# Reordering the scaling of x's last four row tiles, the unread products and one weight split in the modulation stage of a hybrid decoder kernel

## The chip, the cores and the metric

The kernel runs on one core of one Trainium2 chip. The metric is device microseconds of one execution. Before the change, three runs took 1377.65 us in the median (1375.61 to 1378.57).

## The reference, cut to what matters

One decoder layer on x of 1024 rows by 1024 columns, float32. The whole layer feeds on `h`, which the kernel makes first:

```python
mod = jax.nn.silu(c) @ ada_w + ada_b
shift, scale, gate = jnp.split(mod, 3, axis=-1)
h = rms_norm(x, norm_w) * (1 + scale[:, None, :]) + shift[:, None, :]
proj = h @ w_in
...
merged = jax.nn.sigmoid(g_a) * (y_a @ w_proj_a) + jax.nn.sigmoid(g_b) * (y_b @ w_proj_b)
return x + gate[:, None, :] * (merged @ w_out)
```

Between `proj` and `merged` lie a chunked spatial gating mixer and a state space mixer. A last `rms_norm` follows. All that comes after `h` is the same work, in the same order on every engine, before and after the change.

## The kernel before, in words

The change lies in the first stage (some 76 us), which makes `h` transposed, in column blocks of 128, and multiplies each block with the first 288 columns of `w_in` that the kernel wants early.

**Norm of x.** x lies in eight row tiles of 128 rows, x0 to x7. `square(t)` lets ScalarE sum the squares of tile t (one pass over 128x1024, then a readout). `factors(t)` makes the factor 1/sqrt(mean + eps): a small VectorE instruction on one column (L380), then a power on GpSimd (L381). `normed(t, half, V)` multiplies one half of the tile's columns, 128x512, with the factor on VectorE (L388). Half 0 holds columns 0 to 511, half 1 the rest. The factors of x0 to x3 are taken one after the other ahead of the stretch that is changed here.

**Blocks.** There are eight steps n; step n makes block k = KS[n] with KS = (0, 4, 1, 5, 2, 6, 3, 7), so step 0 reads half 0 of x's tiles and step 1 reads half 1. For each block: `matvec(n)` multiplies `scz` (the silu of c) with a block of `ada_w` (the tile `aw`) into `pm`, and a copy makes `row` of it; `modulation(n)` turns the row into two columns with TensorE and adds the constants on VectorE, which gives `md` (shift and scale); `transposes(n, h)` transposes four 128x128 pieces of x's tiles (h = 0: x0 to x3, h = 1: x4 to x7) into one PSUM bank `px`, of which there is one; `rows_of_h(n, h)` makes of it and `md` the block `hf` on ScalarE (L308), a high part of it on ScalarE (L309, the cast) and the low part on VectorE (L313); `split_w0(n)` makes the high and low parts of the early weights (`w0h`, `w0d` on ScalarE, `w0l`, `w0d` on VectorE); and `first_products(n)` multiplies, eight products for each h, numbered 1 to 16 in a step.

**Order.** Everything in this stage is kept in the order of the program on its engine. The dictionary that `prepare(n)` returns says after which product of the step before the parts of step n are issued. For step 1 it reads: after the eighth product of step 0 the second half of block 0 (`transposes(0, 1)`, `rows_of_h(0, 1)`) with `matvec(1)` and `split_w0(1)`; after the eleventh `transposes(1, 1)`, `modulation(1)`, `rows_of_h(1, 1)`; after the sixteenth the other half of block 1.

**Unread products.** `warm(n)` issues n products of two constant tiles into a part of PSUM that nothing reads before it is overwritten. The profile shows each of them, as every 128x128 or 32x256 float32 product, as two records.

**Queues.** All loads go through SyncE's queue in the order of the program: x0 to x3, `aw` and `w0r` of step 0, x4 to x7, `aw` and `w0r` of step 1, five small parameters, then `aw` and `w0r` of steps 2 and on. Two `aw` tiles exist, so the load for step n + 2 waits for `matvec(n)`.

Of the kernel before, what the change touches and what calls it, by code (L numbers as in the profile page):

```python
# [35 lines left out]
def hybrid_kernel(  # L36
# [21 lines left out]
    V, A, G, PE = Engine(nc.vector), Engine(nc.scalar), Engine(nc.gpsimd), nc.tensor  # L58
# [31 lines left out]
    def mm(acc, l, r, first=True, last=True):  # L90
        pin(PE.matmul(acc, l, r, start=first, stop=last))  # L91

    def tp(dst, src, idn):
        pin(PE.transpose(dst, src, idn))  # L94

    def f32(t):
        return t.bitcast(F32)
# [61 lines left out]
    def ax(name, tag="pm"):  # L159
        return psum0.tile([P, 512], F32, name=name, tag=tag, bufs=1)  # L160
# [15 lines left out]
    def wide(name, dt=F32):  # L176
        return w4[0].tile([P, S], dt, name=name, tag="w4", bufs=w4[1])


    with tc.tile_pool(name="p0", bufs=1, reuse_waits="tile") as p0:  # L180
# [14 lines left out]
        def hf_tile(k, h):  # L195
            if k not in hf2:
                hf2[k] = wide(f"hf{k}")
            return hf2[k][:, h * 512 : (h + 1) * 512]
# [31 lines left out]
        def split_w0(n):  # L230
            raw, wd, hi, lo = wk[n]
            pin(A.copy(hi, raw[:, NH:W0]))
            pin(A.copy(wd[:, 0:NH], raw[:, 0:NH]))
            pin(V.tensor_sub(lo, raw[:, NH:W0], f32(hi)))
            pin(V.tensor_sub(wd[:, NH:], raw[:, 0:NH], f32(wd[:, 0:NH])))
# [17 lines left out]
        def warm(n):  # L253

            for _ in range(n):
                mm(accs[2][1][:, 0:P], ident, ones)
# [10 lines left out]
        def matvec(n):  # L267

            pms[n] = pm = ax(f"pm{n}")
            for i in range(KT):  # L270
                q = i % 4
                mm(pm[32 * q : 32 * q + 32, 0:256], scz[:, i, :], aw[n][:, i].rearrange("p j c -> p (j c)"),
                   i < 4, i >= 4)
            row = p0.tile([P, 256], F32, name=f"row{n}", tag="row", bufs=2)
            pin(V.tensor_copy(row, pm[:, 0:256]) if n == 0 else A.copy(row, pm[:, 0:256]))
            mds[n] = row

        def modulation(n):

            k, pm, row = KS[n], pms[n], mds[n]  # L280
            for j in range(2):
                mm(pm[:, 256 + j : 257 + j], row[:, j * P : (j + 1) * P], ones[:, 0:1])
            md = p0.tile([P, 2], F32, name=f"md{n}", tag="md", bufs=3)
            pin(V.tensor_add(md[:, 0:1], pm[:, 256:257], par[:, 16 + k : 17 + k]))
            pin(V.scalar_tensor_tensor(md[:, 1:2], pm[:, 257:258], par[:, 24 + k : 25 + k], par[:, 8 + k : 9 + k],
                                       op0=ALU.add, op1=ALU.mult))
            mds[n] = md

        def transposes(n, h):
            k = KS[n]  # L290
            px = pxs[n, h] if n + h == 0 else ax(f"px{n}_{h}", "px")
            for i in range(4):
                tp(px[:, i * P : (i + 1) * P], xt[4 * h + i][:, k * P : (k + 1) * P], ident)
            pxs[n, h] = px

        def rows_of_h(n, h):
            k, md, px = KS[n], mds[n], pxs[n, h]
            if k < 4 and h:
                b12 = wide(f"b12_{k}", F32R)
                hh, hl = b12[:, 0:512], b12[:, 512:1024]  # L300
            else:
                nm = ("b11" if k < 4 else ("b21", "b22")[h])
                hh, hl = bop[nm][0][k % 4], bop[nm][1][k % 4]
            if n + h:
                hfs[k, h] = hf_tile(k, h)
            hf = hfs[k, h]
            if n + h:
                pin(A.activation(hf, px, AF.Identity, scale=md[:, 1:2], bias=md[:, 0:1]))  # L308
                pin(A.copy(hh, hf))  # L309
            else:  # L310
                pin(V.tensor_scalar(hf, px, md[:, 1:2], md[:, 0:1], op0=ALU.mult, op1=ALU.add))
                pin(V.tensor_copy(hh, hf))
            pin(V.tensor_sub(hl, hf, f32(hh)))  # L313
            hhs[n, h] = (hh, hl)
# [52 lines left out]
        def halves(n):  # L367

            return (0, 1) if KS[n] < 4 else (1, 0)
# [5 lines left out]
        def square(t):  # L375
            pin(A.activation(junk, xt[t], AF.Square, accum_out=sq0[:, t : t + 1]))

        def factors(t):
            bs = slice(t, t + 1)
            pin(V.tensor_scalar(sq0[:, bs], sq0[:, bs], 1.0 / D, EPS, op0=ALU.mult, op1=ALU.add))  # L380
            pin(G.tensor_tensor(rs[:, bs], sq0[:, bs], nhalf[:, bs], op=ALU.pow))  # L381

        def normed(t, half, eng):
            part = xt[t][:, half * 512 : (half + 1) * 512]
            if eng is A:
                pin(A.mul(part, part, rs[:, t : t + 1]))
            else:
                pin(V.tensor_scalar_mul(part, part, rs[:, t : t + 1]))  # L388

        for t in range(4):  # L390
            square(t)
            factors(t)
            normed(t, 0, V)
        transposes(0, 0)
        matvec(0)
        split_w0(0)
# [3 lines left out]
        rows_of_h(0, 0)  # L400
        for t in range(4, NCH):
            square(t)
            factors(t)
            normed(t, 0, V)
            if t in (5, 6):
                normed(t - 5, 1, V)
        for t in range(4, NCH):
            normed(t, 1, V)
        for t in (2, 3):
# [2 lines left out]
        def prepare(n):  # L412

            if n == 1:
                return {
                    8: lambda: (warm(6), transposes(0, 1), rows_of_h(0, 1), matvec(1), split_w0(1), warm(5)),
                    11: lambda: (transposes(1, 1), modulation(1), rows_of_h(1, 1)),
                    16: lambda: (transposes(1, 0), rows_of_h(1, 0)),
                }
            a, b = halves(n)  # L420
            return {
                2: lambda: (matvec(n), transposes(n, a)),
                6: lambda: (modulation(n), rows_of_h(n, a)),
                14: lambda: (transposes(n, b), rows_of_h(n, b)),
            }
# [20 lines left out]
        for n in range(KT):  # L446
            todo = prepare(n + 1) if n + 1 < KT else {}
            for at, _ in enumerate(first_products(n), 1):
                if at == 1 and n + 2 < KT:
                    load_aw(n + 2)  # L450
                    load_w0(n + 2)
                if at == 1 and n == 1:
                    load(dsk, d_skip.to_broadcast([P, NH]))
                if at in todo:
                    todo[at]()
                for f, kk in sums.get((n, at), ()):
                    f(kk)
                if at == 2 and 0 < n < KT - 1:
                    split_w0(n + 1)
                if n == 4 and at == 8:  # L460
                    small_parameters()
# [1357 lines left out]
    n = 0  # L1819
# [284 lines left out]
```

## Time and profile before

| | us |
|---|---|
| three runs, median | 1377.65 |
| profiled execution, its own time | 1379.03 |
| its span, first to last instruction | 1377.3 |
| outside the span | 1.7 |
| TensorE busy in the span | 1358.4 |
| VectorE, ScalarE, GpSimd busy | 1058.2, 788.0, 203.1 |

The profiled execution took 1.4 us more than the median of the three runs and 0.5 us more than the slowest of them. All times in the parts below are counted from the start of its span. A row of the timeline names its start, how long the group lasted, the engine, the line, the operation, the tiles (`px<-ident,x`: px is written, ident and x are read) and how many instructions are in the group; the brackets at its end give the time that the engine stood idle before it, and what ended that. PE is TensorE, DVE VectorE, ACT ScalarE, POOL GpSimd, SP SyncE.

### The profile page before, as it was taken

What the parts mean: (1) busy time and instruction counts of PE and PEld (TensorE: products, weight loads), DVE (VectorE), ACT (ScalarE), POOL (GpSimd) and SP (SyncE); (2) the same over time, 40 slices, a digit from 0 to 9 for tenths busy, and PEclk for the clock granted to TensorE, in tenths of its full rate; (3) what the DMA queues carried; (4) which work ended last, traced back from release to release, by engine and by line L of the source; (5) the groups of instructions that cost most, each with busy time, mean ns of one, the idle gap of its engine ahead of it and who ended that gap; (6) DMA issues with size and microseconds to landing.
All of it is one profiled execution on the core that took longest, in us unless ns stands there. A gap on an engine that the chain in (4) does not pass through costs nothing.

```text
span 1377.3 us, 20335 instructions
## 1 busy us (share of the span) xinstructions
PE 1358.4 (99%) x6947; PEld 1121.2 (81%) x6947; DVE 1058.2 (77%) x1793; ACT 788.0 (57%) x1465; POOL 203.1 (15%) x208
## 2 busy tenths in 40 slices
PE   8999999999999999999999999999999999999998
PEld 6778888888888888888878888888888878888886
DVE  5766766888776687778889988567887887778975
ACT  5764456565656656565556655577877744233543
POOL 1000000000000000000000000006898881000012
PEclk9999999999999999999999999999999999999999
DMA  8665532545323346776887886578989959977733
GB/s 266 169 221 163 173 111 93 166 140 164 107 81 123 107 134 176 210 225 206 249 258 231 245 253 180 168 270 310 327 264 315 313 169 296 392 263 285 258 120 123
DMA packets 272364, 286.58 MB, mean 208 GB/s; under 512 B 18780, under 2 KB 215812, under 8 KB 272260
## 3 DMA queue, kind: packets, MB, share of 16 engines
q1 hardware_dynamic: 196100, 214.35, 49.4%
q10 hardware_dynamic: 76160, 70.92, 15.1%
q8 instruction: 55, 0.90, 0.3%
q14 instruction: 49, 0.40, 0.1%
HBM read 198.77 MB, written 86.44 MB: 207 GB/s over the span
## 4 chain that ended last, share of the span: by engine, by line
PE 80%; DVE 6%; DMA 6%; issue 3%; POOL 2%; ACT 1%; SPq 0%; ACTq 0%; POOLq 0%; DVEq 0%
PE x L1721 6%; PE xuz L591 6%; PE xcb L591 5%; PE xx L591 5%; PE yp L1721 5%; PE pma L91 4%; PE xz L591 4%; PE xg L591 4%; PE ou L1964 3%; PE yuz L591 3%; PE vx L703 3%; PE acc L91 3%; PE ycb L591 3%; PE vy L703 2%; PE yx L591 2%
## 5 line engine op out<-in xcount | busy, mean ns | idle before, releaser
L56 POOL TENSOR_SCALAR_AFFINE_SELECT dcy<-dcy 128x1024 f32<-128x1024 f32 x32 | 34.9, 1092 | 778.5 <-DMA yl<-ya_d 733.1
L56 ACT ACTIVATE dcy<-dcy,nacs 128x128 f32<-128x128 f32 x256 | 78.4, 389 | 17.6 <-POOL dcy L56 17.2
L56 ACT ACTIVATE ea<-dcy 64x512 f32<-64x512 f32 x64 | 40.3, 629 | 8.9 <-DMA dcy<-acs_d 8.5
L91 PE MATMUL pma<-yh,wah 128*128 128x512 f32 x128 | 43.0, 417 | 0.0
L91 PE MATMUL pma<-yh,wal 128*128 128x512 f32 x128 | 42.7, 414 | 0.0
L56 POOL TENSOR_TENSOR yz<-y,sl 128x512 f32<-128x512 f32 x32 | 41.9, 1310 | 0.6
L1043 ACT ACTIVATE ac<-ac 128x1024 f32<-128x1024 f32 x32 | 33.9, 1061 | 12.8 <-DVE ac L1041 12.7
L56 DVE TENSOR_TENSOR ym<-yn,ea 128x512 f32<-128x512 f32 (+1 forms) x32 | 19.9, 623 | 27.6 <-PE yn L91 27.5
L56 DVE TENSOR_TENSOR dcy<-dcy,pc 128x1024 f32<-128x1024 f32 x32 | 38.9, 1215 | 2.4 <-PE pc L94 0.9
L91 PE MATMUL pma<-yl,wah 128*128 128x512 f32 x128 | 39.9, 393 | 0.0
L56 POOL TENSOR_TENSOR y<-y,ym 128x512 f32<-128x512 f32 (+1 forms) x32 | 38.4, 1199 | 9.3 <-DVE ym L56 9.2
L1041 DVE SCALAR_TENSOR_TENSOR ac<-c2cb,cwt,ac 128x1023 f32<-128x1023 f32 (+2 forms) x24 | 30.7, 1280 | 6.8 <-ACT ac L1039 6.7
L1041 DVE SCALAR_TENSOR_TENSOR ac<-c2x,cwt,ac 128x1023 f32<-128x1023 f32 (+2 forms) x24 | 30.7, 1279 | 6.1 <-ACT ac L1039 6.0
L91 PE MATMUL yi<-dcy,xd 128*64 128x128 f32 x512 | 35.0, 279 | 0.3 <-DVE xd L56 0.3
L91 PE MATMUL sp<-xe,bn 128*128 128x256 f32 x112 | 32.7, 409 | 0.0
L91 PEld LDWEIGHTS yi<-dcy,xd 128*64 128x64 f32 x512 | 27.3, 136 | 6.4 <-issue 4.4
L2025 POOL TENSOR_TENSOR r<-r,xr 128x512 f32<-128x512 f32 x4 | 6.3, 1588 | 170.2 <-DMA xr<-in_x_dram 169.0
L1041 DVE SCALAR_TENSOR_TENSOR ac<-c1x,cwt,ac 128x1023 f32<-128x1023 f32 (+2 forms) x24 | 30.7, 1277 | 0.7 <-ACT ac L1039 0.7
L1041 DVE SCALAR_TENSOR_TENSOR ac<-c1cb,cwt,ac 128x1023 f32<-128x1023 f32 (+2 forms) x24 | 30.6, 1276 | 0.0
L56 DVE SCALAR_TENSOR_TENSOR yn<-yn,par,rb 128x512 f32<-128x512 f32 x32 | 25.7, 804 | 6.2 <-DMA yn<-yb_d 6.2
L56 DVE SCALAR_TENSOR_TENSOR y<-sl,dskt,yi 128x256 f32<-128x256 f32 x64 | 27.5, 470 | 1.2 <-POOL yz L56 1.2
L91 PEld LDWEIGHTS pma<-yl,wah 128*128 128x128 f32 x128 | 24.0, 188 | 5.4
(2911 smaller groups left out, 4352.0 us busy)
## 6 DMA issues: line engine op xcount, KB each, us to landing
sl<-s_d SPq DMA_DIRECT2D x32, 768.0 KB
s_d<-ac ACTq DMA_DIRECT2D x32, 512.0 KB
dcy<-acs_d SPq DMA_DIRECT2D x32, 512.0 KB
aw<-in_ada_w_dram SPq DMA_DIRECT2D x16, 512.0 KB
vp<-in_w_in_dram SPq DMA_DIRECT2D x32, 256.0 KB
wbr<-in_w_proj_b_dram SPq DMA_DIRECT2D x64, 128.0 KB
wb_d<-wbb ACTq DMA_DIRECT2D x32, 256.0 KB
wb_d<-wbc ACTq DMA_DIRECT2D x32, 256.0 KB
```

The lines of the kernel that those rows point to most:

```text
L56: return lambda *a, **k: tc.keep_in_program_order(f(*a, **k))
L91: pin(PE.matmul(acc, l, r, start=first, stop=last))
L591: pin(PE.matmul(ps, lw[:, k * P : (k + 1) * P], r[k], start=first and n + k == 0, stop=n == 2 and k == 3, skip_group_check=not first))
L703: pin(PE.matmul(ps[j], l[k][:, js], r, start=first and k + m == 0, stop=k == 3 and m == 2, skip_group_check=not first))
L1041: V.scalar_tensor_tensor(ac[:, s:], cc[:, : S - s], conv_wt[:, 3 - s, i : i + 1], ac[:, s:], op0=ALU.mult, op1=ALU.add)
L1043: A.activation(ac, ac, AF.Silu)
L1721: pin(PE.matmul(ps[j], a[:, v, js], r, start=first and n + k == 0, stop=n == 2 and k == KT - 1, skip_group_check=not first))
L1964: pin(PE.matmul(ps, a[k][v][:, j * P : (j + 1) * P], wop[nm, k][r][:, cs], start=first and n + k == 0, stop=n == 2 and k == 3, skip_group_ ...
L2025: G.tensor_add(rows[j][:, LEFT], rows[j][:, LEFT], xr.pop(j))
```

## The change

Three edits, all in the order of the program.

1. The small instructions (L380 before, L381 now) for x4, x5 and x6 are issued together, with the three powers on GpSimd behind each other. Then come half 1 of x0 and half 0 of x4, x5, x6; then the factor of x7, half 1 of x1, half 0 of x7. The number of scalings is the same.
2. `transposes(0, 1)` gets two unread products ahead of its second, third and fourth transposition. Six unread products ahead of it become four, and the five behind `matvec(1)` go: eleven become ten.
3. `transposes(1, 1)` comes after the tenth product and not after the eleventh, and `split_w0(1)` comes behind `rows_of_h(1, 1)`, so behind the eleventh product and not the eighth.

```diff
-        def transposes(n, h):
+        def transposes(n, h, between=0):
             k = KS[n]
             px = pxs[n, h] if n + h == 0 else ax(f"px{n}_{h}", "px")
             for i in range(4):
+                warm(between if i else 0)
                 tp(px[:, i * P : (i + 1) * P], xt[4 * h + i][:, k * P : (k + 1) * P], ident)
             pxs[n, h] = px
...
         for t in range(4, NCH):
             square(t)
+        for t in (4, 5, 6):
             factors(t)
-            normed(t, 0, V)
-            if t in (5, 6):
-                normed(t - 5, 1, V)
+        for t, half in ((0, 1), (4, 0), (5, 0), (6, 0)):
+            normed(t, half, V)
+        factors(7)
+        normed(1, 1, V)
+        normed(7, 0, V)
         for t in range(4, NCH):
             normed(t, 1, V)
...
             if n == 1:
                 return {
-                    8: lambda: (warm(6), transposes(0, 1), rows_of_h(0, 1), matvec(1), split_w0(1), warm(5)),
-                    11: lambda: (transposes(1, 1), modulation(1), rows_of_h(1, 1)),
+                    8: lambda: (warm(4), transposes(0, 1, 2), rows_of_h(0, 1), matvec(1)),
+                    10: lambda: transposes(1, 1),
+                    11: lambda: (modulation(1), rows_of_h(1, 1), split_w0(1)),
                     16: lambda: (transposes(1, 0), rows_of_h(1, 0)),
                 }
```

The order on three engines shows what moved. First VectorE, from the small instruction of x4's factor on, before the change (sq are the sums of squares, rs the factors, x_242 to x_245 are x4 to x7, x_238 and x_239 are x0 and x1):

```order
L380 TENSOR_SCALAR sq_329<-sq_329 128x1
L388 TENSOR_SCALAR x_242<-x_242,rs 128x512
L380 TENSOR_SCALAR sq_329<-sq_329 128x1
L388 TENSOR_SCALAR x_243<-x_243,rs 128x512
L388 TENSOR_SCALAR x_238<-x_238,rs 128x512
L380 TENSOR_SCALAR sq_329<-sq_329 128x1
L388 TENSOR_SCALAR x_244<-x_244,rs 128x512
L388 TENSOR_SCALAR x_239<-x_239,rs 128x512
L380 TENSOR_SCALAR sq_329<-sq_329 128x1
L388 TENSOR_SCALAR x_245<-x_245,rs 128x512
```

And the same stretch of VectorE now:

```order
L381 TENSOR_SCALAR sq_329<-sq_329 128x1 x3
L389 TENSOR_SCALAR x_238<-x_238,rs 128x512
L389 TENSOR_SCALAR x_242<-x_242,rs 128x512
L389 TENSOR_SCALAR x_243<-x_243,rs 128x512
L389 TENSOR_SCALAR x_244<-x_244,rs 128x512
L381 TENSOR_SCALAR sq_329<-sq_329 128x1
L389 TENSOR_SCALAR x_239<-x_239,rs 128x512
L389 TENSOR_SCALAR x_245<-x_245,rs 128x512
```

Before, each small instruction is followed by the scaling that needs its own power; now a scaling with another, older factor stands between each power and the scaling that needs it.

Then TensorE, from the end of block 0's first eight products to `transposes(1, 1)`, before (acc_237 with ones and ident is the unread product, pm the matvec, b_0_437 the second half of block 0; px_1_432 and px_1_464 are the bank `px` at two uses):

```order
L91 MATMUL acc_237<-ones,ident 128x128 x6
L94 MATMUL px_1_432<-ident,x_242 128x128
L94 MATMUL px_1_432<-ident,x_243 128x128
L94 MATMUL px_1_432<-ident,x_244 128x128
L94 MATMUL px_1_432<-ident,x_245 128x128
L91 MATMUL pm_441<-aw_273,scz 32x256 x8
L91 MATMUL acc_237<-ones,ident 128x128 x5
L91 MATMUL acc_236<-b_0_437,w0h_266 128x512
L91 MATMUL acc_237<-b_0_437,w0h_266 128x512
L91 MATMUL acc_236<-b_0_437,w0l_267 128x512
L94 MATMUL px_1_464<-ident,x_242 128x128
```

And TensorE there now (px_1_430 and px_1_458 are the two uses of the bank):

```order
L91 MATMUL acc_237<-ones,ident 128x128 x4
L94 MATMUL px_1_430<-ident,x_242 128x128
L91 MATMUL acc_237<-ones,ident 128x128 x2
L94 MATMUL px_1_430<-ident,x_243 128x128
L91 MATMUL acc_237<-ones,ident 128x128 x2
L94 MATMUL px_1_430<-ident,x_244 128x128
L91 MATMUL acc_237<-ones,ident 128x128 x2
L94 MATMUL px_1_430<-ident,x_245 128x128
L91 MATMUL pm_445<-aw_273,scz 32x256 x8
L91 MATMUL acc_236<-b_0_441,w0h_266 128x512
L91 MATMUL acc_237<-b_0_441,w0h_266 128x512
L94 MATMUL px_1_458<-ident,x_242 128x128
```

Six unread products now stand between the transpositions, and none stands between the matvec and the products.

Last ScalarE, from the copy of step 1's row on, before (w0h_278 and w0d_277 are the high parts of step 1's early weights, hf_474 is block 1, b22h_188 its cast):

```order
L275 COPY row_450<-pm_441 128x256
L232 CAST w0h_278<-w0r_276 128x256
L233 CAST w0d_277<-w0r_276 128x32
L318 CAST t1h_172<-hf_248 128x512
L308 ACTIVATE hf_474<-px_1_464,md_471 128x512
L309 CAST b22h_188<-hf_474 128x512
```

And ScalarE there now (hf_469 is block 1):

```order
L275 COPY row_454<-pm_445 128x256
L319 CAST t1h_172<-hf_248 128x512
L309 ACTIVATE hf_469<-px_1_458,md_466 128x512
L310 CAST b22h_188<-hf_469 128x512
L232 CAST w0h_278<-w0r_276 128x256
L233 CAST w0d_277<-w0r_276 128x32
```

The two casts of the weights moved behind block 1's first cast; on VectorE the two low parts moved the same way.

## The prediction

> **What bounds the kernel now.** First the page: which engine fills the span.
>
> ```profile
> span 1377.3 us, 20335 instructions
> PE 1358.4 (99%) x6947; PEld 1121.2 (81%) x6947; DVE 1058.2 (77%) x1793; ACT 788.0 (57%) x1465; POOL 203.1 (15%) x208
> ```
>
> TensorE stands idle for 18.9 us in all, so what it gains early comes out at the end unless a later wait eats it. Its two longest waits, by who was waited for (us in total, times, longest):
>
> ```profile
> PE pp L94 <- DMA pk<-in_ada_b_dram: 3.5, 1, 3.5
> PE px L94 <- DVE x L388: 2.3, 2, 1.3
> ```
>
> The second is the place of the change: transpositions wait for VectorE's scalings. TensorE's timeline there:
>
> ```profile
> 20.03 1.50 PE L91 MATMUL acc<-ones,ident 128*128 128x128 f32 x12
> 21.37 0.38 PE L94 MATMUL px<-ident,x 128*128 128x128 f32 x2
> 22.77 0.33 PE L94 MATMUL px<-ident,x 128*128 128x128 f32 x1 [1.01 <-DVE x L388]
> 24.37 0.41 PE L94 MATMUL px<-ident,x 128*128 128x128 f32 x1 [1.28 <-DVE x L388]
> 24.72 1.93 PE L91 MATMUL pm<-aw,scz 128*32 128x256 f32 x16
> 26.58 1.99 PE L91 MATMUL acc<-ones,ident 128*128 128x128 f32 x10
> 28.33 0.71 PE L91 MATMUL acc<-b,w0h 128*128 128x512 f32 x2
> ...
> 29.54 0.50 PE L91 MATMUL pm<-ones,row 128*128 128x1 f32 x4
> ...
> 31.30 0.66 PE L94 MATMUL px<-ident,x 128*128 128x128 f32 x4
> 31.95 0.73 PE L91 MATMUL acc<-b22h,w0h 128*128 128x512 f32 x2
> 32.61 1.07 PE L91 MATMUL pm<-aw,scz 128*32 128x256 f32 x16
> ```
>
> A matvec takes 1.93 us at 24.72, but 1.07 at 32.61. The windows show why: busy us of PE, PEld, DVE, ACT and POOL, then the granted clock, the DMA share and GB/s.
>
> ```profile
> 22.00:23.00 1.00, 0.23 (x1) 0.14 (x1) 0.78 (x2) 0.36 (x1) 0.19 (x1) 1.00 0.45 125
> 23.00:24.00 1.00, 0.09 (x1) 0.00 (x0) 0.34 (x3) 0.00 (x0) 0.55 (x1) 1.00 0.85 240
> 24.00:25.00 1.00, 0.63 (x5) 0.34 (x9) 1.00 (x3) 0.17 (x1) 0.00 (x0) 0.74 1.02 303
> ...
> 27.00:28.00 1.00, 1.00 (x7) 1.00 (x7) 0.63 (x3) 1.00 (x4) 0.00 (x0) 0.55 0.33 110
> ```
>
> Two nearly idle microseconds, and then the clock falls to half: a mean of 0.74 in 24 to 25 puts the fall at 24.5, a mean of 0.55 in 27 to 28 the return at 27.9, 3.4 us later. So TensorE pays twice: for the wait, and for what it runs slowly afterwards.
>
> **Part one, the scalings.** The rows of VectorE, GpSimd and ScalarE that set when x7 is scaled:
>
> ```profile
> 18.59 0.15 DVE L380 TENSOR_SCALAR sq<-sq 128x1 f32<-128x1 f32 x1
> 19.40 0.49 DVE L388 TENSOR_SCALAR x<-x,rs 128x512 f32<-128x512 f32 x1 [0.66 <-POOL rs L381]
> ...
> 23.83 2.07 DVE L388 TENSOR_SCALAR x<-x,rs 128x512 f32<-128x512 f32 x5 [0.66 <-POOL rs L381]
> ```
>
> ```profile
> 18.82 0.55 POOL L381 TENSOR_TENSOR rs<-sq,nhalf 128x1 f32<-128x1 f32 x1 [6.56 <-DVE sq L380]
> ```
>
> ```profile
> 18.84 0.18 ACT L376 ACTIVATION_READ_ACCUMULATOR junk<-x 128x1 f32 x1
> 19.99 1.06 ACT L376 ACTIVATE junk<-x 128x1024 f32<-128x1024 f32 x1 [0.96 <-DMA x<-in_x_dram]
> 20.95 0.19 ACT L376 ACTIVATION_READ_ACCUMULATOR junk<-x 128x1 f32 x1
> ```
>
> Each tile costs 0.81 us from the small instruction to the scaling (18.59 to 19.40), and the chains run one behind the other: x7's sum is read out by 21.14, but x7 is scaled only from 23.83 to 24.32. Now x6's sum (19.02) lets the three small instructions end near 19.2; the three powers follow each other from 18.82 at 0.55 to about 20.5; half 1 of x0, x4, x5 and x6 are scaled by 21.0 (0.40 apart, as the five rows in 2.07 show). x7's small instruction can go at 21.17, 0.03 behind its readout, and its scaling 0.81 later, at 21.98, done at 22.46; half 1 of x1 fits between. That is 1.85 us earlier. Its floor is x7's arrival at 19.99, which the change doesn't touch.
>
> **Part two, the unread products.** Twelve rows of six products last 1.50: 0.25 a product. TensorE now issues four (20.03 to 21.03), a transposition (0.12 to 0.16, from 0.66 for four), and three times two products and a transposition: x7's begins at 20.03 + 1.00 + 3 x 0.62 = 22.89, so the products, not VectorE, decide here, by 0.4 us. It began at 24.37: 1.48 earlier. TensorE has no hole in that stretch, so I take the clock as whole.
>
> ScalarE goes on from there:
>
> ```profile
> 24.82 0.78 ACT L308 ACTIVATE hf<-px,md 128x512 f32<-128x512 f32 x1 [2.46 <-PE px L94]
> 25.64 0.62 ACT L309 CAST b<-hf 128x512 fp32r<-128x512 f32 x1
> ...
> 26.98 0.41 ACT L232 CAST w0h<-w0r 128x256 fp32r<-128x256 f32 x1
> 27.29 0.22 ACT L233 CAST w0d<-w0r 128x32 fp32r<-128x32 f32 x1
> 27.41 0.62 ACT L318 CAST t1h<-hf 128x512 fp32r<-128x512 f32 x1
> 30.46 0.78 ACT L308 ACTIVATE hf<-px,md 128x512 f32<-128x512 f32 x1 [2.44 <-PE acc L91]
> ```
>
> Before, the cast was ready at 26.26, yet the product began at 28.33: matvec and five unread products stood ahead. Now: transposition 22.89 + 0.33, hf at 23.27, cast 24.09 to 24.71, product at 24.77; the matvec (1.07 from 23.0) is out of the way. The gain of 3.56 has three terms: half clock, 1.93 - 1.07 for the matvec and 1.75 - 1.25 for ten rows of unread products, 1.36; the products behind the matvec, which at full clock would end at 26.97 against the cast's 26.32, 0.65; the earlier transposition, the rest, 1.55.
>
> Matvec(1) needs its aw, queued behind x7. From 19.99, its 1.05 MB (128 x 2048 float32) at the 240 GB/s of the window 23 to 24 are in by 24.4; at worst the matvec ends at 25.4 and the gain shrinks by 0.65. I take nothing: the queue was moving all along, so aw's start was before 19.99. Matvec(1)'s earlier end also releases the load of step 3's aw sooner; nothing new stands ahead of it in SyncE's queue.
>
> The page "TensorE: Matmul & The Clock Gate" of the Trainium skill, in its table "Why this matters for your kernels", warns only of gaps over about 3 us between bursts. Here the gaps were 1.01 and 1.28 us with single transpositions around them, and the clock fell; the measurement decides. By that rule the 1.36 would not belong in the sum, which would come to 1.84.
>
> **Part three, the order behind it.** Transpositions(1, 1) move one product forward and modulation stays behind three: the way from the first product to px's next use was 31.30 - 28.33 = 2.97. Now: two products 0.47, four transpositions 0.45, one product 0.24, modulation at 25.93; from there the old 0.92 to hf (29.54 to 30.46) and 0.78 + 0.06 to the bank's release: 27.69. Gain 3.61.
>
> Then comes the cost. The two weight casts were hidden in a gap of ScalarE; now they stand between b22h's cast and the next hf, and the first product of step 1 needs w0h. Start to start they hold ScalarE 0.31 + 0.12, so b22h's product loses 0.31: 3.30 left. On VectorE the same move costs:
>
> ```profile
> 27.42 0.43 DVE L234 TENSOR_TENSOR w0l<-w0r,w0h 128x256 fp32r<-128x256 f32 x1 [0.32 <-ACT w0h L232]
> 27.77 0.18 DVE L235 TENSOR_TENSOR w0d<-w0r,w0d 128x32 fp32r<-128x32 f32 x1
> 28.06 0.69 DVE L319 TENSOR_TENSOR t1l<-hf,t1h 128x512 fp32r<-128x512 f32 x1
> ```
>
> 0.35 to 0.64 by the starts; the last start followed t1h's end at 28.03, so I take 0.43. It sits in VectorE's dense run of step 1, whose end gives step 2's md: 3.61 - 0.43 = 3.2 left.
>
> **The sum.** 3.2 us, with the same work behind it on every engine. Loads behind this stage start when buffers come free, so they move along. The profiled execution would take 1379.03 - 3.2 = 1375.8. It lies 1.4 over the median; from the median the forecast is 1377.65 - 3.2 = 1374.45, said as 1374.5.
>
> **The rivals.** *Half clock was rare before* (0.35). If most executions before ran this stretch at full clock, 1.36 goes from the gain: 1.84, or 1375.8. Three runs spread over 2.96 us, so something differs by more than that between runs; against it, the only trace shows the fall. The same page, in "Part 1: The HAM clock gate", says the window in which TensorE's activity is judged runs free of the kernel's start, so that the same kernel comes out differently from run to run; no trace here shows two phases. By it this rival would hold in part of the runs.
>
> *The gain is given back* (0.11). A wait that doesn't move takes 3.2 us later, say a load whose time is fixed: about 1377.6. Against it: of TensorE's two longest waits only the first is for a DMA, at the very start.
>
> *The half clock moves* (0.05). Between 24.0 and 28.7 there is now no unread product, a hole of 0.7 us ahead of the first product, and 0.3 ahead of the transpositions at 27.7. If that counts as idle, half clock falls on the products behind: each stretch of 3.4 us like the one seen costs at most 1.7. From two such stretches on, the gain is gone; three give 5.1 - 3.2 = 1.9 slower, 1379.5. For it: the 0.32 us of busy time between 22 and 24 were too little. Against: between 24.0 and 28.7 TensorE would be about three quarters busy.
>
> **How the numbers follow.** The forecast has 0.49. The range takes in both likely cases, 1374.5 and 1375.8, each with about 1.0 to 1.5 for the runs' spread (half of 2.96): 1372.9 to 1376.8; the other two rivals, 0.16, lie outside. A measurement of this kernel tells 0.2% from no change, 2.76 us. The forecast passes that by 0.4, in about two of three measurements; the first rival in one of four: 0.33 + 0.09 = 0.42 faster. Slower by over 0.2% takes more than the third rival's price: 0.03. The rest, 0.55, is within 0.2%.
>
> **What would show it.** Right: no half clock between 20 and 30; x7's transposition at 22.9, not waiting for VectorE; the product of b at 24.8 (28.33); the transpositions at 27.7 (31.30); b22h's product at 28.6 (31.95). Wrong: a clock of 0.50 anywhere in 20 to 32; matvec(1) waiting for aw; b's product later than 25.7; or the shift of 3 us there at 32 and no longer at 76.

## The result and the profile after

The changed kernel took 1373.19 us in the median of 7 runs (1371.61 to 1375.06), the kernel before 1377.69 (1375.61 to 1381.16): a ratio of 0.9965, with a 95% interval of 0.9956 to 0.9975. That is 4.5 us faster by the medians. The number lies in the forecast's range, 1.3 us below the 1374.5 that was forecast; the outcome that the forecast thought likeliest, a difference within 0.2%, did not come. Three single runs far outside the rest (7819 us of the kernel before, 1506 and 1698 us of the version told below that moves the split alone) are left out of every ratio here.

The page of the changed kernel, the same two lines as before:

```profile
span 1371.5 us, 20331 instructions
PE 1355.6 (99%) x6945; PEld 1120.9 (82%) x6945; DVE 1057.7 (77%) x1793; ACT 789.4 (58%) x1465; POOL 205.8 (15%) x208
```

The wait of the transpositions for VectorE (2.3 us before) is no longer among TensorE's waits. Two small ones stand there instead:

```profile
PE acc L91 <- ACT b L310: 0.5, 1, 0.5
...
PE acc L91 <- ACT w0h L232: 0.3, 1, 0.3
```

TensorE's timeline in the stretch of the change:

```profile
23.39 0.61 PE L91 MATMUL acc<-ones,ident 128*128 128x128 f32 x4
23.98 0.33 PE L94 MATMUL px<-ident,x 128*128 128x128 f32 x1
24.24 1.07 PE L91 MATMUL pm<-aw,scz 128*32 128x256 f32 x16
25.83 0.73 PE L91 MATMUL acc<-b,w0h 128*128 128x512 f32 x2 [0.52 <-ACT b L310]
...
28.82 0.66 PE L94 MATMUL px<-ident,x 128*128 128x128 f32 x4
29.77 0.73 PE L91 MATMUL acc<-b22h,w0h 128*128 128x512 f32 x2 [0.30 <-ACT w0h L232]
```

The matvec lasts 1.07 and not 1.93, and it starts right behind x7's transposition. The product of b starts as soon as the cast is there. b22h's product waits 0.30 for w0h, the price of the moved split. Now the windows, as shown of before (TensorE's busy time first, the granted clock third from the end):

```profile
22.00:23.00 1.00, 1.00 (x11) 1.00 (x11) 0.94 (x3) 0.82 (x2) 0.33 (x2) 1.00 0.28 82
23.00:24.00 1.00, 1.00 (x10) 0.83 (x9) 0.56 (x2) 0.00 (x0) 0.40 (x1) 1.00 0.54 155
24.00:25.00 1.00, 1.00 (x17) 0.53 (x17) 1.00 (x3) 0.66 (x1) 0.00 (x0) 1.00 1.05 313
25.00:26.00 1.00, 0.48 (x9) 0.17 (x2) 1.00 (x3) 0.97 (x3) 0.00 (x0) 1.00 0.83 234
...
27.00:28.00 1.00, 1.00 (x8) 0.87 (x8) 0.77 (x3) 0.02 (x1) 0.00 (x0) 1.00 1.07 328
```

The hole at 22 to 24 is filled; what is left are the 0.52 us ahead of the product of b and the 0.30 ahead of b22h's. The clock is whole in every window from 20 to 32.

VectorE, GpSimd and ScalarE show what the forecast had not seen:

```profile
19.84 0.27 DVE L381 TENSOR_SCALAR sq<-sq 128x1 f32<-128x1 f32 x3
20.02 0.48 DVE L389 TENSOR_SCALAR x<-x,rs 128x512 f32<-128x512 f32 x1
20.94 1.60 DVE L389 TENSOR_SCALAR x<-x,rs 128x512 f32<-128x512 f32 x3 [0.44 <-POOL rs L382]
22.45 0.15 DVE L381 TENSOR_SCALAR sq<-sq 128x1 f32<-128x1 f32 x1
22.52 0.48 DVE L389 TENSOR_SCALAR x<-x,rs 128x512 f32<-128x512 f32 x1
23.44 2.07 DVE L389 TENSOR_SCALAR x<-x,rs 128x512 f32<-128x512 f32 x5 [0.44 <-POOL rs L382]
```

```profile
20.06 1.95 POOL L382 TENSOR_TENSOR rs<-sq,nhalf 128x1 f32<-128x1 f32 x3 [7.46 <-DVE sq L381]
22.68 0.72 POOL L382 TENSOR_TENSOR rs<-sq,nhalf 128x1 f32<-128x1 f32 x1 [0.67 <-DVE sq L381]
```

```profile
20.45 1.06 ACT L377 ACTIVATE junk<-x 128x1024 f32<-128x1024 f32 x1 [1.14 <-DMA x<-in_x_dram]
21.41 0.19 ACT L377 ACTIVATION_READ_ACCUMULATOR junk<-x 128x1 f32 x1
```

x7's sum was read out at 21.60, but its small instruction ran only at 22.45: it stands in VectorE's order behind x6's scaling, which waited for the third of three powers (1.95 us for three). And x7's own power took 0.72 us, where each power of the kernel before took 0.55. So x7 was scaled at 23.44, 2.99 us after its arrival at 20.45. Before it was 3.84, the forecast had 1.99.

In this execution everything started later: TensorE's first instruction at 4.13, where it had been 3.46, and x7 came 0.46 later. Measured from the start of the span, b22h's product moved from 31.95 to 29.77, by 2.2 us only, while the span shrank by 5.8. The two traces therefore don't add up by themselves: one stage varies from run to run, and so does what follows it. The experiments take that apart.

### The profile page after: what moved, and what is told of

The parts are those of the page before. It is cut to its first block, busy times and chain, and to the rows that moved or that the text cites. A ratio compares the mean times of both kernels' runs of the same rounds, so it can differ in the third digit from the quotient of the medians.

```text
span 1371.5 us, 20331 instructions
## 1 busy us (share of the span) xinstructions
PE 1355.6 (99%) x6945; PEld 1120.9 (82%) x6945; DVE 1057.7 (77%) x1793; ACT 789.4 (58%) x1465; POOL 205.8 (15%) x208
## 4 chain that ended last, share of the span: by engine, by line
PE 93%; DVE 2%; issue 1%; DMA 1%; ACT 1%; POOL 1%; SPq 0%; ACTq 0%; POOLq 0%; DVEq 0%
PE x L1726 6%; PE xcb L596 6%; PE xuz L596 6%; PE xx L596 6%; PE xz L596 6%; PE xg L596 5%; PE pma L91 5%; PE yp L1726 5%; PE ou L1969 3%; PE yuz L596 3%; PE vx L708 3%; PE ycb L596 3%; PE yz L596 3%; PE yx L596 3%; PE acc L91 3%; PE yg L596 3%
## 5 line engine op out<-in xcount | busy, mean ns | idle before, releaser
L56 DVE TENSOR_TENSOR ym<-yn,ea 128x512 f32<-128x512 f32 (+1 forms) x32 | 19.9, 623 | 27.2 <-PE yn L91 27.1
```

The costliest lines, as they stand in the source:

```text
L56: return lambda *a, **k: tc.keep_in_program_order(f(*a, **k))
```

## The experiments

Two theories. **A**: the whole gain is made in the first stage, and half clock costs the kernel before more than the first trace showed. **B**: part of the gain is made later, where the kernel before has waits of its own. The runs of the kernel before that stand beside each experiment had medians from 1377.6 to 1378.2 us.

### The kernel before again

No edit.

> The kernel before, unchanged, timed against itself, with a second trace of it. Both theories: within 0.1% of the kernel before. What its trace tells: theory A (the change's gain is the shortening of the first stage; TensorE's waits behind 500 us come and go from run to run) expects another set of waits behind 500 us than the first trace's, their sum differing by 1 us or more; theory B (the later waits of the kernel before are its own, and the change takes some of them away) expects the same waits at 533, 699, 788 and 1053 us, of 0.5 to 1.1 us each. Rival on the clock (half clock was rare): no half clock between 20 and 32 us here; the forecast: half clock again.

Measured: 1.0002 of the kernel before (0.9993 to 1.0011). The windows of its trace:

```profile
24.00:25.00 1.00, 0.01 (x1) 0.00 (x0) 0.34 (x3) 0.00 (x0) 0.55 (x1) 1.00 1.06 316
25.00:26.00 1.00, 0.71 (x9) 0.43 (x13) 1.00 (x4) 0.34 (x1) 0.00 (x0) 1.00 0.74 200
26.00:27.00 1.00, 1.00 (x13) 0.48 (x6) 1.00 (x4) 0.97 (x3) 0.00 (x0) 0.69 1.06 328
...
28.00:29.00 1.00, 1.00 (x7) 1.00 (x7) 1.00 (x4) 0.30 (x1) 0.00 (x0) 0.50 0.77 202
```

Half clock again, after the same hole, but from 26.4 (0.69 in 26 to 27) to 29.8, and not from 24.5. The matvec all but escapes (1.17 us); the unread products behind it and those of b pay. From x7's transposition to b22h's first product it takes as long as in the first trace, though: 7.59 us here, 7.58 (24.37 to 31.95) there.

```profile
25.29 0.33 PE L94 MATMUL px<-ident,x 128*128 128x128 f32 x1 [1.28 <-DMA aw<-in_ada_w_dram]
...
32.88 0.72 PE L91 MATMUL acc<-b22h,w0h 128*128 128x512 f32 x2
```

Behind 500 us the waits are other ones: the one at 533 is gone, and TensorE stands idle for 1.62 us ahead of xg at 699 where it was 0.92. So these two changed without any edit, as theory A has it.

### The three edits alone

The first edit alone (the order of the scalings):

```diff
+        for t in (4, 5, 6):
             factors(t)
-            normed(t, 0, V)
-            if t in (5, 6):
-                normed(t - 5, 1, V)
+        for t, half in ((0, 1), (4, 0), (5, 0), (6, 0)):
+            normed(t, half, V)
+        factors(7)
+        normed(1, 1, V)
+        normed(7, 0, V)
```

> Only the first edit, the order of VectorE's small instructions and scalings; unread products and the split of the weights as in the kernel before. x7 scaled about 3.0 us after it arrives, where it was 3.84. If the clock still falls in the waits: gain 0.8 us in the stage. If the shorter waits keep it whole: 0.8 + 1.4 = 2.2. Theory A: the time moves by just that. Theory B: up to 2 us more.

Measured: 0.9976 (0.9967 to 0.9984), 3.3 us, with single runs from 1373.4 to 1378.3. Its trace has a whole clock; one transposition still waits 1.06 us. The gain is a microsecond more than the 2.2 us expected with a whole clock.

The second edit alone (the unread products):

```diff
-                    8: lambda: (warm(6), transposes(0, 1), rows_of_h(0, 1), matvec(1), split_w0(1), warm(5)),
+                    8: lambda: (warm(4), transposes(0, 1, 2), rows_of_h(0, 1), matvec(1), split_w0(1)),
```

> Only the second edit, the unread products between the transpositions and none behind the matvec. x7's scaling is as late as in the kernel before, so the gain is the clock, 1.36 us, and the products behind the matvec, 0.65: 2.0 us if the six products between the transpositions keep the clock whole; 0.65 if they don't. Theory A: the time moves by just that. Theory B: up to 2 us more.

Measured: 0.9977 (0.9967 to 0.9986), 3.2 us; 2.0 had been expected. In its trace:

```profile
24.37 0.33 PE L94 MATMUL px<-ident,x 128*128 128x128 f32 x1 [0.83 <-DVE x L389]
24.63 1.07 PE L91 MATMUL pm<-aw,scz 128*32 128x256 f32 x16
26.22 0.73 PE L91 MATMUL acc<-b,w0h 128*128 128x512 f32 x2 [0.52 <-ACT b L310]
```

x7's transposition starts at 24.37, exactly when it did before, so nothing came from the scalings; the product of b starts at 26.22 instead of 28.33. That is the clock and the removed products, 2.1 us, as expected; but the kernel gained a microsecond more.

The third edit alone (the later transpositions and the split):

```diff
-                    8: lambda: (warm(6), transposes(0, 1), rows_of_h(0, 1), matvec(1), split_w0(1), warm(5)),
-                    11: lambda: (transposes(1, 1), modulation(1), rows_of_h(1, 1)),
+                    8: lambda: (warm(6), transposes(0, 1), rows_of_h(0, 1), matvec(1), warm(5)),
+                    10: lambda: transposes(1, 1),
+                    11: lambda: (modulation(1), rows_of_h(1, 1), split_w0(1)),
```

> Only the third edit, the second set of transpositions one product earlier and the split of step 1's weights behind block 1's first cast. By the working of the forecast it costs 0.3 to 0.4 us in the stage and gains nothing: +0.3 us, inside the noise. If the time fell by 1 us or more, the later order on ScalarE and VectorE would be what the forecast missed.

Measured: 1.0004 (0.9995 to 1.0012): inside the noise, as expected. Its trace tells something else:

```profile
23.00:24.00 1.00, 0.00 (x0) 0.00 (x0) 0.37 (x1) 0.00 (x0) 0.55 (x1) 0.84 0.62 159
24.00:25.00 1.00, 0.83 (x5) 0.39 (x9) 1.00 (x4) 0.32 (x1) 0.00 (x0) 0.50 1.01 289
...
29.00:30.00 1.00, 1.00 (x4) 0.70 (x4) 0.00 (x0) 0.00 (x0) 0.00 (x0) 0.50 1.13 342
30.00:31.00 1.00, 1.00 (x9) 0.95 (x7) 0.00 (x0) 0.00 (x0) 0.00 (x0) 0.74 1.18 317
```

Half clock from 23.7 (0.84 in 23 to 24) to 30.5, 6.8 us, twice as long as in the first trace. So its price is not one number.

### The clock alone

The kernel before with six more unread products between the transpositions, the other eleven kept:

```diff
-                    8: lambda: (warm(6), transposes(0, 1), rows_of_h(0, 1), matvec(1), split_w0(1), warm(5)),
+                    8: lambda: (warm(6), transposes(0, 1, 2), rows_of_h(0, 1), matvec(1), split_w0(1), warm(5)),
```

> The kernel before with six more unread products, two ahead of the second, third and fourth transposition, and all eleven others kept: the scalings stay as late as they were, so this changes the clock alone. By the forecast's term 1.36 us, 1376.8 (0.9990). Theory A: the clock is worth more than the first trace had it, 2 to 2.5 us (0.9983), since a stretch of half clock falls on other work in other runs and can last twice as long. No half clock between 20 and 35 us.

Measured: 0.9982 (0.9973 to 0.9991), 2.5 us by the ratio, with a whole clock in its trace. More work on TensorE makes the kernel faster. The forecast's 1.36 (0.9990) lies at the edge of the interval. The trace prices the clock directly, as this kernel runs the same instructions from x7's transposition on as the kernel before:

```profile
24.61 0.33 PE L94 MATMUL px<-ident,x 128*128 128x128 f32 x1 [0.83 <-DVE x L389]
...
27.01 0.71 PE L91 MATMUL acc<-b,w0h 128*128 128x512 f32 x2
...
30.62 0.74 PE L91 MATMUL acc<-b22h,w0h 128*128 128x512 f32 x2
```

It takes 6.01 us to b22h's first product, where both traces of the kernel before took 1.57 us more.

### The changed kernel again, and with a delay

> The changed kernel again, with a second trace. Both theories: 0.9965 of the kernel before, some 1373.4 us. Theory A (the whole gain is made in the first 38 us, since half clock costs the kernel before more than the 1.36 us of the first trace; from there to the end the two kernels take the same within a spread of some 2 us from run to run): the time from step 1's last set of transpositions to the end of the span lies within the spread of the six traces so far, 1336.4 to 1339.9 us. Theory B (the change takes away later waits): it lies near 1336.4 again.

Measured: 0.9963 (0.9950 to 0.9976). The time from step 1's last set of transpositions to the end was 1338.3 (1372.0 - 33.75), in the middle of theory A's spread. Its first stage started earlier than in the first trace of the change, and it meets the forecast's times:

```profile
22.58 0.33 PE L94 MATMUL px<-ident,x 128*128 128x128 f32 x1
23.30 1.07 PE L91 MATMUL pm<-aw,scz 128*32 128x256 f32 x16 [0.39 <-DMA aw<-in_ada_w_dram]
24.43 0.74 PE L91 MATMUL acc<-b,w0h 128*128 128x512 f32 x2
...
27.42 0.66 PE L94 MATMUL px<-ident,x 128*128 128x128 f32 x4
28.38 0.73 PE L91 MATMUL acc<-b22h,w0h 128*128 128x512 f32 x2 [0.30 <-ACT w0h L232]
```

Forecast were 22.9, 24.8, 27.7 and 28.6. The matvec waits 0.39 us for its aw, and that costs nothing, as the cast of b ends only at 24.4 and the matvec is over by then.

The changed kernel with eleven unread products behind the matvec:

```diff
-                    8: lambda: (warm(4), transposes(0, 1, 2), rows_of_h(0, 1), matvec(1)),
+                    8: lambda: (warm(4), transposes(0, 1, 2), rows_of_h(0, 1), matvec(1), warm(11)),
```

> The changed kernel with eleven unread products behind the matvec, 11 x 0.25 us, of which 0.52 fill the hole there: the first stage ends 2.2 us later, about where the kernel before ends it, with a whole clock. Theory A: 2.2 us slower than the changed kernel, 0.998 of the kernel before, and the rest of the kernel as long as ever. Theory B (the later waits come with the shift): all of the gain is lost, 0.9995 to 1.000.

Measured: 0.9990 (0.9981 to 0.9998), a median of 1376.51, 3.2 us above the changed kernel's 1373.3. Between the two theories, nearer to B. The next experiments take it up.

### The first stage by itself

Five kernels were cut off behind the last early product. Left out is all that follows; the sums are copied over half of x's tiles and these are stored, which is the same in all five. The order inside the stage is unchanged.

```diff
                 if n == 4 and at == 8:
                     small_parameters()
-
+        for t in range(NCH):
+            V.tensor_copy(xt[t][:, 0:512], accs[1 + t % 2][t // 4])
+        for t in range(NCH):
+            move(out[t * P : (t + 1) * P, :], xt[t])
```

The kernel before:

> The kernel before, cut off behind its first stage: all that follows the last early product is left out; the sums are copied over half of x's tiles on VectorE and the tiles stored. The order inside the stage is unchanged. It measures the first stage alone, with the clock of each run. Theory A (the whole gain is made in the stage): the cut kernels differ by what the whole ones do, 4.5 us or so between before and changed. Theory B (part of the gain is made later): they differ by 2.7 to 3.2 us, and some 1.5 us of the gain comes behind the stage.

The changed kernel:

> The changed kernel, cut off in the same place in the same way. Theory A: 4.5 us below the cut kernel before. Theory B: 2.7 to 3.2 us below it.

The kernel before with the clock kept whole:

> The kernel before with six more unread products between the transpositions (the clock alone, as timed whole), cut off behind the first stage. The forecast's term: 1.36 us below the cut kernel before. If half clock costs more in most runs than in the first trace: 2 to 3 us below.

The version with three further edits, told below:

> The changed kernel with x7's small instruction ahead of x6's scaling, one unread product between the transpositions and the split ahead of block 1's rows, cut off behind the first stage. By the stage's own rows 0.5 to 0.8 us below the cut changed kernel; as timed whole it was about 1 us above the changed kernel. If it is below here, the difference of the whole kernels lay in how the rest fell out; if it is above here, in the stage (the clock or the arrival of x7).

And the changed kernel with the delay:

> The changed kernel with eleven more unread products behind the matvec, cut off behind the first stage. Whole it was 3.2 us above the changed kernel. By its rows the stage should end 2.2 us later than that of the cut changed kernel, 87.8 us; if it ends 3.2 later, the stage alone accounts for it.

| cut kernel | runs | median us | lowest to highest | to the changed kernel | whole kernels, by medians |
|---|---|---|---|---|---|
| before | 6 | 89.27 | 87.43 to 90.88 | +3.72 | +4.5, +4.7, +4.2 |
| before, clock kept | 4 | 87.55 | 87.05 to 88.25 | +2.00 | +1.6 |
| changed | 5 | 85.55 | 85.31 to 86.14 | | |
| changed, with the delay | 4 | 88.65 | 87.63 to 88.82 | +3.10 | +3.2 |
| three further edits | 4 | 85.21 | 85.10 to 85.79 | -0.34 | +1.2 |

The cut kernel before varies by 4% from run to run; that spread is what is measured here, and all six runs stand in the table. The windows of its trace, taken in the run of 90.88, show a cause:

```profile
23.00:24.00 1.00, 0.33 (x1) 0.14 (x1) 0.47 (x3) 0.41 (x1) 0.45 (x1) 1.00 0.30 88
24.00:25.00 1.00, 0.33 (x1) 0.18 (x1) 0.87 (x3) 0.00 (x0) 0.10 (x1) 0.68 0.58 166
...
30.00:31.00 1.00, 1.00 (x5) 0.70 (x5) 0.00 (x0) 0.00 (x0) 0.00 (x0) 0.50 0.94 275
31.00:32.00 1.00, 1.00 (x9) 0.96 (x8) 0.17 (x2) 0.00 (x0) 0.00 (x0) 0.90 1.01 307
```

Half clock from 24.4 to 31.2, 6.8 us. And TensorE, with the product of b at 29.10 and `transposes(1, 0)`, whose time the forecast gave, at 33.05:

```profile
24.67 0.48 PE L94 MATMUL px<-ident,x 128*128 128x128 f32 x1 [1.28 <-DVE x L388]
25.08 1.93 PE L91 MATMUL pm<-aw,scz 128*32 128x256 f32 x16
26.94 2.50 PE L91 MATMUL acc<-ones,ident 128*128 128x128 f32 x10
29.10 1.20 PE L91 MATMUL acc<-b,w0h 128*128 128x512 f32 x2
...
33.05 0.66 PE L94 MATMUL px<-ident,x 128*128 128x128 f32 x4
33.70 0.74 PE L91 MATMUL acc<-b22h,w0h 128*128 128x512 f32 x2
```

The cut changed kernel reaches the two at 24.75 and 27.74:

```profile
22.91 0.33 PE L94 MATMUL px<-ident,x 128*128 128x128 f32 x1
...
24.75 0.73 PE L91 MATMUL acc<-b,w0h 128*128 128x512 f32 x2 [0.35 <-ACT b L310]
...
27.74 0.65 PE L94 MATMUL px<-ident,x 128*128 128x128 f32 x4
28.69 0.72 PE L91 MATMUL acc<-b22h,w0h 128*128 128x512 f32 x2 [0.30 <-ACT w0h L232]
```

So the stage gives 3.7 us, of which the medians put 1.7 down to the clock (before to clock kept, 89.27 to 87.55) and 2.0 to the rest. From b22h's first product to the end of the span all five traces take 55.1 to 55.2 us: what differs in the cut kernels is made ahead of it.

The time from x7's transposition to b22h's first product tells what half clock costs:

| kernel | trace | half clock, us | us |
|---|---|---|---|
| before, clock kept | whole; cut | none | 6.01; 6.02 |
| before | first; again | 3.4; 3.4 | 7.58; 7.59 |
| before | cut | 6.8 | 9.03 |
| changed | first; second; third; cut | none | 5.79; 5.80; 5.79; 5.78 |

So 3.4 us of half clock cost 1.57, and 6.8 us cost 3.0. That fits the six runs of the cut kernel before. With the clock kept, the median is 87.55; one such stretch would make it 89.1, two 90.6. The six lie at 87.43, at 89.05 to 89.33 (three), and at 90.11 and 90.88. Only the last was traced, so for the other five this is an estimate. Their listed mean clock can't decide it, since it counts the half clock behind the last product too.

x7's transposition itself starts at 24.2 to 25.4 in the seven traces with the old order of scalings (24.70 in the mean), and at 22.6 to 24.1 in seven with the new one and two unread products between (23.40). That is 1.3 us, where the forecast had 1.48, and it varies by as much from run to run.

The delay cost 3.1 us in the stage, not the 2.2 that was worked out, and 3.2 whole. The rows of the traces still say 2.1 to 2.2: from x7's transposition to b22h's first product the delayed kernel takes 7.84 us cut and 8.00 whole, the changed one 5.78 and 5.80. The other 0.9 between the two cut traces lies ahead of the delay, in x7's transposition, which came at 23.83 and not at 22.91. Whether the medians differ by 3.1 for that reason is not shown. But the stage and the whole agree, and so the rest of the kernel did not answer to the shift. That speaks for theory A.

### The changed kernel a third time

> The changed kernel a third time. Cut off behind the first stage, before and changed differ by 3.7 us, whole by 4.5 to 4.7. If the 0.8 to 1 us between is chance, more runs bring the whole difference towards 3.7 (0.9973 of the kernel before); if it belongs to the kernel, it stays at 4.5 to 5 (0.9965).

Measured: 0.9972 (0.9962 to 0.9983), 3.9 us by the ratio. The stage's 3.7 us would be 0.9973 of the whole, which lies in the interval of each of the three measurements.

### A shorter stage that made no faster kernel

```diff
-        for t, half in ((0, 1), (4, 0), (5, 0), (6, 0)):
+        for t, half in ((0, 1), (4, 0), (5, 0)):
             normed(t, half, V)
         factors(7)
+        normed(6, 0, V)
         normed(1, 1, V)
...
-                    8: lambda: (warm(4), transposes(0, 1, 2), rows_of_h(0, 1), matvec(1)),
+                    8: lambda: (warm(4), transposes(0, 1, 1), rows_of_h(0, 1), matvec(1)),
...
-                    11: lambda: (modulation(1), rows_of_h(1, 1), split_w0(1)),
+                    11: lambda: (modulation(1), split_w0(1), rows_of_h(1, 1)),
```

> The changed kernel with x7's small instruction one scaling earlier (ahead of x6's scaling, not behind it), one unread product and not two between the transpositions, and step 1's split behind modulation(1), ahead of block 1's rows. In the changed kernel's trace x7's small instruction stood ready at 21.60 and ran at 22.45, behind a scaling that waited for GpSimd; and b22h's first product waited 0.30 us for w0h. Theory A: 0.5 us from the first, 0.3 from the second, some 0.8 us faster than the changed kernel (0.9959 of the kernel before) if the clock stays whole; slower than it by 1 to 2 us if fewer unread products let it fall.

Measured: 0.9978 (0.9969 to 0.9986), 1.2 us above the changed kernel by the medians, and not below it; the cut stage was shorter by 0.34. Then the last of these edits alone:

> The changed kernel with step 1's split ahead of block 1's rows, nothing else. By the rows of the stage 0.3 us below the changed kernel, 1372.9. If what follows the stage depends on the kernel, it may come out above, at 1374.5 as the version with three edits did.

Measured: 0.9972 (0.9963 to 0.9982), the same as the changed kernel. And the other two alone:

> The changed kernel with x7's small instruction ahead of x6's scaling and one unread product between the transpositions, the split where the changed kernel has it. By the rows of the stage 0 to 0.3 us below the changed kernel. If fewer unread products let the clock fall in some runs, 1 to 2 us above it in these.

Measured: 0.9982 (0.9972 to 0.9991), a median of 1375.15 and a highest run of 1377.48. So the split costs nothing that can be measured, and what is lost comes with the other two. Their highest runs (1378.53 with all three, 1377.48 here) and that of the first edit alone (1378.29), where fewer or no products stand between the transpositions, go beyond anything in 20 runs of the changed kernel (highest 1375.06). That would fit a clock that falls in some runs, but no trace caught one. And two kernels with all six products between have such runs too: 1379.04 with the clock kept, at a mean clock of 0.997 where the nine others have 0.998 or 0.999, and 1380.25 with the delay, at 0.998. So the cause stays open. No whole version beat the changed kernel.

## Why the forecast was off

**What bounds the kernel, and the place of the hole.** Right. Filling it, and nothing else, made the kernel faster (the clock alone, 0.9982), and TensorE's wait for VectorE, 2.3 us before, is gone in the first two traces of the change and 0.3 in the third.

**The scalings.** Right in kind, mis-sized in the first trace. The forecast had x7 scaled 1.99 us after arrival; it was 2.99, since the small instruction stood behind a scaling that waited for a power, which cost 0.8, and from it to the scaling took 0.99 and not 0.81. The forecast took both chains at 0.55 a power; three in a row took 1.95 and not 1.65, and x7's own took 0.72. The unread products hid 0.4 of it. In the second trace it was 2.17 (arrival at 19.87, scaling at 22.04; the power is the difference). There the products decided as forecast, x7's transposition came at 22.58, and the forecast's chain of times held to 0.4 us at each point. That the times themselves were met there is in part luck: x7 arrived about when the forecast took it to (19.99), and not at 20.45 as in the first trace.

**The clock.** Here is the step that failed. The prediction put it as "half clock, 1.93 - 1.07 for the matvec and 1.75 - 1.25 for ten rows of unread products, 1.36", worked out from one execution with 3.4 us of half clock, and put 0.35 on half clock being rare before. Both made the gain too small. In that very execution the price was 1.57 (7.58 against 6.01): x7's transposition ran slowly as well, and at a whole clock the ten rows take 1.14 us from start to start (25.87 to 27.01) and not 1.25. In two of the four traces half clock lasted 6.8 us, which cost 3.0 in the one that can be compared. In these traces the length decided and not the place: the second trace of the kernel before had its 3.4 us on other instructions, and paid the same. Timed, the term is 1.7 us by the cut kernels and 2.5 (1.2 to 3.7) by the whole ones. With these in the place of 1.36 the sum of 3.2 becomes 3.6 to 4.3; the rest of it, 1.84, was 2.0 in the cut kernels. At 3.2 the forecast stood only 0.4 above the 2.76 that it took for 0.2%, and so it held "within 0.2%" for likelier than faster.

**The rival "half clock was rare before"** had 0.35, and it was wrong. Half clock came in each of the four traces with the old scalings and no products between. Among the 93 runs of the kernel before that stand beside the experiments, 11 have a mean clock of 0.999; they took 1376.3 us in the mean, the other 82 took 1378.2. That difference, 1.9 us, has the size of the clock's price, though a mean over the whole span doesn't say where the clock fell. This rival held most of the chance that was put on "within 0.2%"; without it the forecast would have said faster. The page "TensorE: Matmul & The Clock Gate" of the Trainium skill, quoted there from its "Part 1: The HAM clock gate", says that the window runs free of the kernel's start. The traces agree: against the start of x7's transposition (24.17, 24.67, 24.37 and 25.29), half clock began 0.5 and 0.3 us before it and 0.1 and 1.1 us behind it. Where it began before, it lasted 6.8 us, and where behind, 3.4; four traces are few for a rule.

**The order behind it.** Right: alone it makes no difference that can be measured (1.0004), and b22h's product waits 0.30 for w0h where 0.31 was forecast. Matvec(1) did wait for its aw, 0.39 and 0.27 us in the second and third traces of the change, which the prediction named as a sign of being wrong. It cost nothing, as the prediction took it: the cast of b was ready no earlier than the matvec was done.

**The other rivals.** The gain was not given back, and the half clock did not move: the trace of the change has it only behind the last product.

**What stays open.** The whole kernels differ by 3.9 to 5.1 us by the three ratios, the stages by 3.7. Each of the three intervals holds 3.7. Taken together, though, the 20 runs of the changed kernel lie 4.7 below the 93 of the kernel before in the mean (1373.2 and 1377.9). The stage's 3.7 rests on six and five runs, and the six spread over 3.5, so chance may be enough to explain the microsecond between; or it is gained behind the stage. What follows step 1's last set of transpositions took 1339.9 and 1339.1 us in the two traces of the kernel before, and 1336.4 to 1338.3 in the eleven other whole traces. That leans to theory B. But two of the eleven are the kernel before with the third edit alone (1337.5) and with the clock kept (1336.5), and the two executions at the top (1379.03 and 1379.14) were themselves slower by 1.1 than the kernel's mean.

## What to carry to other kernels

A hole on TensorE of 2.3 us, even broken by a single transposition, cost 1.6 to 3.0 us more in the clock afterwards; work that nobody reads, put inside the hole and not only in front of it, was worth 1.7 us in the stage and 2.5 whole. Price such a term over several executions, since a single trace shows one length of it. Where a stage is short and the kernel long, cutting the kernel behind the stage turns a 0.3% question into a 4% one. And where the instructions between two marks are the same, the time from one to the other in several traces prices the clock without the rest.

## What the runs showed of the hardware

Half clock lasted 3.4 us in two traces and 6.8 in two others, and began up to 1.6 us apart against the same transposition. It cost 1.57 us where it lasted 3.4, and 3.0 in the one trace with 6.8 that can be compared.

In the four traces in which the clock fell, TensorE ran nothing but single transpositions for 3.1 to 3.3 us (21.5 to 24.7 in the first), with no idle gap above 1.28. In the trace of the first edit alone that stretch was 2.1 us (21.5 to 23.6), with a gap of 1.06, and the clock stayed whole. No run tells whether the gaps or the whole stretch decide.

Two unread products (0.5 us) between single transpositions of 0.1 us kept the clock whole in every trace that had them. In the old order, where VectorE stands waiting for each power, a power on GpSimd (one column) takes 0.55 us. In the new order, where a scaling runs on VectorE beside it, x7's takes 0.72 to 0.77, and three in a row took up to 1.96; that VectorE's work is the cause is not shown. x7's arrival moved between 19.9 and 21.1 us from one execution to the next.
